# Ordering a four-layer decoder trunk on a different build-time simulation: one block around the whole trace

## The chip, the cores and the metric

The kernel runs on one core of one Trainium2 chip. The metric is the device time of one execution in microseconds (us). A time of a kernel is the median of several runs; beside it stands one profiled execution, whose trace gives a start, a duration and the releasing event of every instruction. The engines are named as the profile names them: PE (TensorE, matrix multiply), PEld (its weight load), DVE (VectorE), ACT (ScalarE), POOL (GpSimd) and SP (SyncE, which here only issues transfers). Each engine works through its own list of instructions strictly in the order of the list. Engines wait for one another by semaphores.

## The reference

A causal trunk of four layers over x of 1024 positions by 1024 channels, f32. Every layer computes `x + gate * mixer(rmsnorm(x) * (1 + scale) + shift)`, where shift, scale and gate come from `c @ ada_w[i] + ada_b[i]`. The mixers:

- layers 0 and 3: HGRN2, a gated linear recurrence with 8 heads of 128 channels. One input projection (1024 to 4096: q, f, i, z), the recurrence in chunks, an RMS norm per head, a SiLU gate, one output projection;
- layer 1: sliding-window attention (window 128), 16 query heads and 4 key heads of 64 channels, rotary embedding, QK norm, a learned sink per head, SiLU gate, output projection;
- layer 2: gated DeltaNet (GDN), 16 value heads and 8 query/key heads of 128 channels, a causal convolution of 4 taps on q, k and v, a triangular solve per chunk, norm, SiLU gate, output projection.

```
h = rmsnorm(x, norm_g[i]) * (1.0 + scale) + shift
y = (hgrn2_mixer, swa_mixer, gdn_mixer)[i % 3](h, ...)
x = x + gate * y
```

## The kernel before

**Tiling.** Everything lies channels-first: a tile has 128 channels on the partitions and 512 positions (a "half", `hf`) along the row. Each f32 operand of a big product is split in a high and a low part of a rounded type (`hi`, `lo`), and `mm3` (L215 to L220) makes one product of three matmuls: hi by hi (L218), lo by hi (L219) and hi by lo (L220). `load_w` (L176) brings a piece of a weight matrix: a transfer that SP issues into `w_raw` (L187, 3 buffers), a cast on ACT to `w_hi` (L189 or L192, 4 buffers), a subtraction on DVE to `w_lo` (L190 or L193, 4 buffers). A block of 128 output columns (`proj_fm`, tile `proj_ps`) takes two such pieces and eight products in each half. The output projections are `out_mm` (tile `outp_ps`, operands loaded by `out_load`: L1306 and L1310 issue transfers on POOL, L1314 casts `o_hi` on ACT, L1315 makes `o_lo` on DVE) and `rest` (tile `out_ps`, residual add at L572).

**Stages and loops.** A start stage (constants, x, modulation of layer 0), and then per layer the mixer over its heads or units and the output projection. HGRN2 goes over 8 heads (`mix` at L1101 has the short matmuls `lev_ps`, `o_ps`, `s_ps`), the attention over 4 groups, GDN over 8 units of two value heads. A GDN unit has an `inverse` (L787): chunk products `kk_ps` and `qk_ps`, a forward substitution of 31 steps on DVE (L837, L838), and four groups of small matmuls in `z_ps` (L866, L874 to L876, L883, L891) between which POOL copies 32-partition blocks (L860, L861, L870, L886); a `scan` over eight chunks (`ks_ps`, `w_ps`, `S_ps`), and `finish`. Beside these run the input projections of later heads or units, and a stream `side` with the modulation (`ada`) of the next layers.

**What sets the order.** `weave` (L66) draws instructions from two to four streams in shares of hand-given costs, so a program order arises. With it each instruction gets a priority number, its place in the program; `high_priority(offset=...)` moves what it encloses that many places ahead (150 for HGRN2's mix, 200 for the attention's, 150 for GDN's scan and inverse, 4000 for `burst`). `tied` (L148) and `issue_after` fix that certain instructions follow others on their engine.

This is not yet the order of the chip. When the kernel function has ended, Tile (the layer that places tiles, chooses the order and writes the semaphores) plays the whole trace once on a timing simulation. Whenever an engine of that simulation can take an instruction, Tile gives it the one with the best priority among those whose inputs and whose tile buffer are there at that simulated moment, also when a better one will be ready a little later. What each engine was given, in that sequence, is its list on the chip, and the chip doesn't deviate from it. Tile has two such simulations: CoreSim, the default, and TimelineSim, which its text calls the more detailed one, with the remark that CoreSim leaves out the fixed cost of GpSimd's elementwise instructions. Before the change every list was made on CoreSim.

Also decided by this play is which buffer of a tile's ring an allocation gets and, with that, which release a transfer waits for.

Of the kernel before, what the change touches and what calls it, by code (L numbers as in the profile page):

```python
# [10 lines left out]
F32 = mybir.dt.float32  # L11
# [9 lines left out]
P = 128  # L21
T = 1024
D = 1024
KT = D // P
HT = 512
NC = HT // P
# [21 lines left out]
def drain(g):  # L48
    for _ in g:
        pass  # L50


def chain(*gs):
    for g in gs:
        yield from g


def take(g, n):
    for _ in range(n):
        c = next(g, None)  # L60
        if c is None:
            return
        yield c
# [1481 lines left out]
@with_exitstack  # L1545
def trunk(ctx: ExitStack, tc: tile.TileContext, x, c, positions, hgrn_lb, ada_w, ada_b, norm_g,
          hg_in_w, hg_out_w, hg_onorm, sw_in_w, sw_out_w, sw_qnorm, sw_knorm, sw_sinks,
          gd_in_w, gd_out_w, gd_conv_w, gd_a_log, gd_dt_bias, gd_onorm, out, layers=(0, 1, 2, 3)):
    ins = dict(x=x, c=c, positions=positions, hgrn_lb=hgrn_lb, ada_w=ada_w, ada_b=ada_b, norm_g=norm_g,
               hg_in_w=hg_in_w, hg_out_w=hg_out_w, hg_onorm=hg_onorm, sw_in_w=sw_in_w, sw_out_w=sw_out_w,  # L1550
               sw_qnorm=sw_qnorm, sw_knorm=sw_knorm, sw_sinks=sw_sinks, gd_in_w=gd_in_w, gd_out_w=gd_out_w,
               gd_conv_w=gd_conv_w, gd_a_log=gd_a_log, gd_dt_bias=gd_dt_bias, gd_onorm=gd_onorm)
    k = Trunk(ctx, tc, ins)
    k.open_norm()
    with tc.tile_pool(name="start", bufs=1, reuse_waits="tile") as sp:
        k.setup(sp)

        x1 = [sp.tile([P, D], F32, name="x_in", tag="x_in1", bufs=NC) for _ in range(NC)]
        sq = sp.tile([P, D], F32, name="x_sq")
        x0 = [sp.tile([P, D], F32, name="x_in", tag="x_in0", bufs=NC) for _ in range(NC)]  # L1560
        k.fetch_x(0, x0)
        ada = []
        for part, bank, col in ((2, ("lev", "ada_row", 2), 0), (0, None, D), (3, ("s", "ada_row", 1), None), (1, None, None)):
            acc = sp.tile([P, HT], F32, name="ada_acc", tag="acc", bufs=3)
            ada.append((layers[0], part, acc, k.ada_load(layers[0], part), bank))
            if layers[0] == 0 and col is not None:
                k.preload(hg_in_w[0], (col,))
        rb = k.norm_stats(0, k.load_x(sp, 0, x0, sq))
        a = k.norm_apply(layers[0], 0, rb)
        for n in range(2):  # L1570
            gs = [k.ada_first(*x) for x in ada[2 * n:2 * n + 2]]
            for g in gs:
                next(g)
            k.step = k.step if n else None
            for g in gs:
                drain(g)
            drain(take(a, KT // 2))
        drain(a)
        k.start = [tc.cur_priority]
        k.fetch_x(1, x1)  # L1580
        ssq = k.load_x(sp, 1, x1, sq)
        k.spill_x(0)
        rb = k.norm_stats(1, ssq)
        k.start.append(tc.cur_priority)
        drain(k.norm_apply(layers[0], 1, rb))
        k.conv_taps(sp)
    k.level_masks()
    k.nst.close()
    for n, i in enumerate(layers):
        nxt = layers[n + 1] if n + 1 < len(layers) else None  # L1590
        k.more = nxt is not None
        side = iter(())
        if n == 0:
            side = k.ada(i, (4, 5))
        if nxt is not None:
            side = chain(side, k.ada(nxt, (0, 1, 2)), k.ada(nxt, (3, 4, 5)))
        body = (k.hgrn2, k.swa, k.gdn)[i % 3](i, side)
        for hf, t in enumerate(body):
            drain(t)
            if nxt is None:  # L1600
                k.store_x(out, hf)
            else:
                if hf == 0:
                    k.open_norm()
                a = k.norm_apply(nxt, hf, k.norm_stats(hf))
                if hf == 0:
                    drain(a)
                else:
                    k.last = a
                    k.nst.close()  # L1610


# [27 lines left out]
```

## Time and profile before

| | |
|---|---|
| median of 3 runs | 2654.2 us (2652.76 to 2654.95) |
| profiled execution, whole | 2652.67 us |
| its span, first to last instruction | 2650.9 us |
| instructions | 50785 |
| busy: PE / PEld | 2563.2 us (97%) / 2045.3 us (77%) |
| busy: DVE / ACT / POOL | 2021.3 (76%) / 1325.2 (50%) / 162.3 us (6%) |
| mean clock granted to TensorE | 0.991 |
| moved by transfers | 309.96 MB, mean 117 GB/s |

The stages in the span, read from the lines that are at work: start 0 to 72 us, HGRN2 of layer 0 to about 520, attention to about 1030, GDN from about 1100 to 2110 with its eight units until about 1910, HGRN2 of layer 3 to the end.

In a row of groups stand line, engine, operation, output<-inputs, count, then busy time and the mean of one in ns, then the idle time just before these instructions and what ended it. In a row of waits stand the waiting engine and line, what it waited for, and total, number and longest in us. In a row of windows stand the stretch, its length, and per engine busy us (number of instructions), then the granted clock, the share of the transfer engines and GB/s. Matmuls are pipelined: one counts as busy until its modelled end, while the next has long started.

### The profile page before, as it was taken

How to read it: one execution, taken by the hardware profiler on the slowest of the kernel's cores; microseconds unless marked ns; L12 is line 12 of the kernel's file. 1: busy time of each engine (PE TensorE's matmuls, PEld its weight loads, DVE VectorE, ACT ScalarE, POOL GpSimd, SP SyncE). 2: the span in 40 equal slices, each digit the busy share in tenths (PEclk: the TensorE clock that was granted, in tenths of full speed). 3: DMA queues.
4: the chain of work that ended last, by engine and by line, in shares of the span. 5: the costliest groups of instructions: out<-in, count | busy, mean ns of one | idle time of the engine just before them, and what ended most of it. 6: DMA issues, size and time to landing. Idle time of an engine off the chain costs nothing.

```text
span 2650.9 us, 50785 instructions
## 1 busy us (share of the span) xinstructions
PE 2563.2 (97%) x18271; PEld 2045.3 (77%) x18271; DVE 2021.3 (76%) x5655; ACT 1325.2 (50%) x3467; POOL 162.3 (6%) x382
## 2 busy tenths in 40 slices
PE   7999999999999999999999999999999999999998
PEld 4777777778888867777777787778788877787777
DVE  5585789777687878868899999988776837368675
ACT  4443444443464655545666666666544434245452
POOL 0001000011000000101001101110221000000010
PEclk8999999999999999999999999999999999999999
DMA  7333343544233252434343444334585312122343
GB/s 263 96 114 92 112 143 118 163 137 138 65 103 104 70 165 90 131 110 117 97 116 90 119 116 120 81 96 104 175 248 173 115 49 80 41 81 66 122 140 116
DMA packets 388369, 309.96 MB, mean 117 GB/s; under 512 B 74851, under 2 KB 314902, under 8 KB 388118
## 3 DMA queue, kind: packets, MB, share of 16 engines
q1 hardware_dynamic: 375574, 265.82, 33.9%
q0 software_dynamic: 12544, 40.90, 4.8%
q8 instruction: 144, 2.36, 0.4%
q14 instruction: 107, 0.88, 0.1%
HBM read 245.75 MB, written 60.88 MB: 116 GB/s over the span
## 4 chain that ended last, share of the span: by engine, by line
PE 73%; DVE 13%; DMA 5%; ACT 4%; issue 3%; SPq 1%; POOL 0%; DVEq 0%; ACTq 0%; POOLq 0%
PE proj_ps L220 10%; PE proj_ps L218 10%; PE proj_ps L219 10%; PE outp_ps L219 5%; PE outp_ps L218 5%; PE outp_ps L220 5%; PE projw_ps L219 2%; PE projw_ps L218 2%; PE projw_ps L220 2%; DVE gd_tb L690 1%; DVE w_lo L190 1%; PE projt_ps L219 1%; PE projt_ps L220 1%; PE projt_ps L218 1%; PE w_ps L945 1%
## 5 line engine op out<-in xcount | busy, mean ns | idle before, releaser
L218 PE MATMUL proj_ps<-hhi,w_hi 128*128 128x512 f32 x1664 | 675.2, 406 | 3.6 <-ACT gd_tb L688 3.3
L219 PE MATMUL proj_ps<-hlo,w_hi 128*128 128x512 f32 x1664 | 671.3, 403 | 0.0
L220 PE MATMUL proj_ps<-hhi,w_lo 128*128 128x512 f32 x1664 | 670.7, 403 | 0.0
L218 PEld LDWEIGHTS proj_ps<-hhi,w_hi 128*128 128x128 f32 x1664 | 314.3, 189 | 64.2 <-ACT gd_tb L688 5.9
L220 PEld LDWEIGHTS proj_ps<-hhi,w_lo 128*128 128x128 f32 x1664 | 314.0, 189 | 57.9 <-issue 0.4
L219 PEld LDWEIGHTS proj_ps<-hlo,w_hi 128*128 128x128 f32 x1664 | 314.4, 189 | 54.9 <-issue 0.9
L189 ACT CAST w_hi<-w_raw 128x512 fp32r<-128x512 f32 x352 | 214.2, 613 | 265.2 <-PE proj_ps L219 155.2
L190 DVE TENSOR_TENSOR w_lo<-w_raw,w_hi 128x512 fp32r<-128x512 f32 x352 | 236.3, 676 | 139.7 <-ACT w_hi L189 136.4
L218 PE MATMUL outp_ps<-o_hi,w_hi 128*128 128x512 f32 x576 | 229.8, 401 | 8.4 <-ACT o_hi L1314 7.1
L219 PE MATMUL outp_ps<-o_lo,w_hi 128*128 128x512 f32 x576 | 229.7, 399 | 1.5 <-DVE o_lo L1315 1.4
L220 PE MATMUL outp_ps<-o_hi,w_lo 128*128 128x512 f32 x576 | 228.4, 398 | 2.6 <-DVE w_lo L190 2.5
L192 ACT ACTIVATE w_hi<-w_raw,par 128x512 fp32r<-128x512 f32 (+1 forms) x136 | 94.9, 698 | 131.4 <-PE outp_ps L219 92.8
L690 DVE SCALAR_TENSOR_TENSOR gd_tb<-gd_xs,taps,gd_tb 128x512 f32<-128x512 f32 x192 | 145.6, 758 | 16.6 <-ACT gd_tb L688 12.4
L218 PEld LDWEIGHTS outp_ps<-o_hi,w_hi 128*128 128x128 f32 x576 | 109.5, 190 | 31.9 <-ACT o_hi L1314 8.7
L444 DVE SCALAR_TENSOR_TENSOR ada_acc<-ada_w,par,ada_acc 128x512 f32<-128x512 f32 x154 | 114.9, 746 | 20.6 <-DMA ada_w<-in_ada_w_dram 19.5
L193 DVE SCALAR_TENSOR_TENSOR w_lo<-w_raw,par,w_hi 128x512 fp32r<-128x512 f32 (+1 forms) x136 | 96.7, 715 | 43.3 <-ACT w_hi L192 40.1
L220 PEld LDWEIGHTS outp_ps<-o_hi,w_lo 128*128 128x128 f32 x576 | 109.6, 190 | 25.7 <-DVE w_lo L190 3.1
L219 PEld LDWEIGHTS outp_ps<-o_lo,w_hi 128*128 128x128 f32 x576 | 109.7, 190 | 25.2 <-DVE o_lo L1315 3.4
L1306 POOL DMA_DIRECT2D o_in<-od x72 | 38.8, 539 | 1216.7 <-DVE hg_F L1177 428.3
L219 PE MATMUL projt_ps<-w_lo,hhi 128*128 128x256 f32 x384 | 110.8, 290 | 2.1 <-DVE w_lo L190 2.1
L218 PE MATMUL projt_ps<-w_hi,hhi 128*128 128x256 f32 x384 | 110.5, 290 | 2.0 <-ACT w_hi L189 2.0
L220 PE MATMUL projt_ps<-w_hi,hlo 128*128 128x256 f32 x384 | 110.7, 290 | 0.0
(411 smaller groups left out, 5336.4 us busy)
## 6 DMA issues: line engine op xcount, KB each, us to landing
ada_w<-in_ada_w_dram SPq DMA_DIRECT2D x160, 256.0 KB, 2.8
w_raw<-in_hg_in_w_dram SPq DMA_DIRECT2D x136, 256.0 KB, 2.8
w_raw<-in_gd_in_w_dram SPq DMA_DIRECT2D x128, 256.0 KB, 2.9
o_in<-od POOLq DMA_DIRECT2D x72, 256.0 KB, 3.5
x<-xd SPq DMA_DIRECT2D x64, 256.0 KB, 4.5
w_raw<-in_gd_out_w_dram SPq DMA_DIRECT2D x64, 256.0 KB, 3.2
xd<-x POOLq DMA_DIRECT2D x48, 256.0 KB, 2.7
w_raw<-in_sw_in_w_dram SPq DMA_DIRECT2D x48, 256.0 KB, 3.0
```

The lines of the kernel that those rows point to most:

```text
L189: nc.scalar.copy(hi, raw)
L190: nc.vector.tensor_tensor(lo, raw, hi.bitcast(F32), ALU.subtract)
L192: nc.scalar.activation(hi, raw, AF.Copy, scale=scale)
L193: nc.vector.scalar_tensor_tensor(lo, raw, scale, hi.bitcast(F32), ALU.mult, ALU.subtract)
L218: mm(out, a[0], b[0], start=start, stop=False)
L219: mm(out, a[0], b[1], start=False, stop=False)
L220: mm(out, a[1], b[0], start=False, stop=stop)
L444: self.step = self.nc.vector.scalar_tensor_tensor(acc, w, c, acc, ALU.mult, ALU.add)
L690: last = nc.vector.scalar_tensor_tensor(y, xs[:, j:j + HT], w(j), y, ALU.mult, ALU.add)
L945: nc.tensor.matmul(po[:, hd[a]], dd["u"][a, hf][:, cs], rhs, start=True, stop=True)
L1306: nc.gpsimd.dma_start(t, od[(k0 + k) * P:(k0 + k + 1) * P, sl])
```

## The change

The body of `trunk` from the creation of the `Trunk` object to the last store is put inside `with tc.block(schedule_with_timeline_sim=True):`. A Tile block is traced into a basic block of its own that is entered unconditionally and ordered as a unit; with this argument Tile plays that block on TimelineSim instead of CoreSim. No instruction of the program's own is added, removed or altered, no priority, offset, share, buffer count or tie is altered, and nothing is left outside the block but the constants that are set before `trunk` is called.

```diff
-    k = Trunk(ctx, tc, ins)
-    k.open_norm()
-    with tc.tile_pool(name="start", bufs=1, reuse_waits="tile") as sp:
-        k.setup(sp)
...
+    with tc.block(schedule_with_timeline_sim=True):
+        k = Trunk(ctx, tc, ins)
+        k.open_norm()
+        with tc.tile_pool(name="start", bufs=1, reuse_waits="tile") as sp:
+            k.setup(sp)
...
+            body = (k.hgrn2, k.swa, k.gdn)[i % 3](i, side)
+            for hf, t in enumerate(body):
+                drain(t)
+                if nxt is None:
+                    k.store_x(out, hf)
                 else:
-                    k.last = a
-                    k.nst.close()
+                    if hf == 0:
+                        k.open_norm()
+                    a = k.norm_apply(nxt, hf, k.norm_stats(hf))
+                    if hf == 0:
+                        drain(a)
+                    else:
+                        k.last = a
+                        k.nst.close()
```

All other lines of the diff are the same lines, indented by four more columns.

More of the change, by code (lines that the diff above doesn't have):

```diff
@@ L1552, in trunk @@
                gd_conv_w=gd_conv_w, gd_a_log=gd_a_log, gd_dt_bias=gd_dt_bias, gd_onorm=gd_onorm)
-    k = Trunk(ctx, tc, ins)
-    k.open_norm()
-    with tc.tile_pool(name="start", bufs=1, reuse_waits="tile") as sp:
-        k.setup(sp)
[L1558 to L1586, printed above, removed]
@@ L1587, in trunk @@
-    k.level_masks()
-    k.nst.close()
[L1589 to L1607, printed above, removed]
-                else:
-                    k.last = a
-                    k.nst.close()
+    with tc.block(schedule_with_timeline_sim=True):
[3 more added lines that the diff above has]
+            k.setup(sp)
+            x1 = [sp.tile([P, D], F32, name="x_in", tag="x_in1", bufs=NC) for _ in range(NC)]
+            sq = sp.tile([P, D], F32, name="x_sq")
+            x0 = [sp.tile([P, D], F32, name="x_in", tag="x_in0", bufs=NC) for _ in range(NC)]
+            k.fetch_x(0, x0)
+            ada = []
+            for part, bank, col in ((2, ("lev", "ada_row", 2), 0), (0, None, D), (3, ("s", "ada_row", 1), None), (1, None, None)):
+                acc = sp.tile([P, HT], F32, name="ada_acc", tag="acc", bufs=3)
+                ada.append((layers[0], part, acc, k.ada_load(layers[0], part), bank))
+                if layers[0] == 0 and col is not None:
+                    k.preload(hg_in_w[0], (col,))
+            rb = k.norm_stats(0, k.load_x(sp, 0, x0, sq))
+            a = k.norm_apply(layers[0], 0, rb)
+            for n in range(2):
+                gs = [k.ada_first(*x) for x in ada[2 * n:2 * n + 2]]
+                for g in gs:
+                    next(g)
+                k.step = k.step if n else None
+                for g in gs:
+                    drain(g)
+                drain(take(a, KT // 2))
+            drain(a)
+            k.start = [tc.cur_priority]
+            k.fetch_x(1, x1)
+            ssq = k.load_x(sp, 1, x1, sq)
+            k.spill_x(0)
+            rb = k.norm_stats(1, ssq)
+            k.start.append(tc.cur_priority)
+            drain(k.norm_apply(layers[0], 1, rb))
+            k.conv_taps(sp)
+        k.level_masks()
+        k.nst.close()
+        for n, i in enumerate(layers):
+            nxt = layers[n + 1] if n + 1 < len(layers) else None
+            k.more = nxt is not None
+            side = iter(())
+            if n == 0:
+                side = k.ada(i, (4, 5))
+            if nxt is not None:
+                side = chain(side, k.ada(nxt, (0, 1, 2)), k.ada(nxt, (3, 4, 5)))
+            body = (k.hgrn2, k.swa, k.gdn)[i % 3](i, side)
[3 more added lines that the diff above has]
+                    k.store_x(out, hf)
+                else:
+                    if hf == 0:
+                        k.open_norm()
+                    a = k.norm_apply(nxt, hf, k.norm_stats(hf))
+                    if hf == 0:
+                        drain(a)
+                    else:
+                        k.last = a
+                        k.nst.close()
```

## The prediction

> **What bounds the kernel now.** I read the page first: busy times and the chain that ended last.
>
> ```profile
> span 2650.9 us, 50785 instructions
> PE 2563.2 (97%) x18271; PEld 2045.3 (77%) x18271; DVE 2021.3 (76%) x5655; ACT 1325.2 (50%) x3467; POOL 162.3 (6%) x382
> PE   7999999999999999999999999999999999999998
> DVE  5585789777687878868899999988776837368675
> PE 73%; DVE 13%; DMA 5%; ACT 4%; issue 3%; SPq 1%; POOL 0%; DVEq 0%; ACTq 0%; POOLq 0%
> ```
>
> PE is busy in nine tenths or more of 38 of 40 slices, and 73% of the chain that ended last are its matmuls. So the time is PE's work, plus the places where the next matmul in PE's list was not ready. What a new order can change are those places. The view by stretches says where they are (length, then PE, PEld, DVE, ACT, POOL):
>
> ```profile
> 0.00:72.00 72.00, 52.46 (x192) 30.89 (x193) 43.57 (x128) 33.06 (x57) 3.22 (x42) 0.87 0.74 267
> 72.00:480.00 408.00, 402.02 (x3550) 318.67 (x3549) 301.24 (x955) 167.91 (x437) 7.25 (x8) 1.00 0.38 115
> 480.00:520.00 40.00, 33.96 (x381) 25.19 (x380) 29.00 (x105) 19.25 (x46) 3.81 (x7) 0.96 0.42 136
> ...
> 570.00:660.00 90.00, 84.54 (x526) 73.75 (x525) 72.11 (x148) 38.72 (x69) 6.74 (x13) 1.00 0.38 117
> ...
> 1030.00:1120.00 90.00, 87.04 (x429) 67.65 (x428) 75.89 (x166) 53.97 (x124) 7.79 (x22) 0.98 0.33 98
> ...
> 1360.00:1850.00 490.00, 479.96 (x3405) 384.52 (x3404) 449.78 (x1325) 318.52 (x1018) 41.14 (x106) 1.00 0.40 105
> 1850.00:1910.00 60.00, 55.46 (x445) 42.56 (x444) 40.80 (x81) 33.90 (x88) 14.66 (x29) 0.94 0.53 158
> ...
> 2110.00:2500.00 390.00, 386.45 (x3479) 306.69 (x3478) 244.22 (x860) 156.41 (x418) 0.00 (x0) 1.00 0.22 68
> 2500.00:2590.00 90.00, 86.55 (x637) 68.26 (x635) 65.13 (x179) 42.00 (x96) 7.53 (x14) 0.98 0.41 134
> 2590.00:2651.00 61.00, 53.93 (x263) 43.93 (x262) 31.34 (x47) 15.24 (x24) 0.00 (x0) 0.99 0.37 123
> sum 2651.00, PE 2563.17 PEld 2045.28 DVE 2021.25 ACT 1325.20 POOL 162.29; mean PE 170.88 PEld 136.35 DVE 134.75 ACT 88.35 POOL 10.82
> ```
>
> PE's idle time is 2651.0 - 2563.2 = 87.8 us. Of it 19.5 lie in the start, where the transfer engines are 74% busy and the data sets the pace. The steady stages have little: 6.0 in layer 0's heads, 10.0 in GDN's units, 3.6 in layer 3's heads. The handovers between mixer and output projection have much for their length: 6.0 in 480 to 520, 5.5 in 570 to 660, 3.0 in 1030 to 1120, 4.5 in 1850 to 1910, 3.5 in 2500 to 2590; then 7.1 at the end.
>
> Two things follow. What an order can win is bounded by 87.8 - 19.5 = 68.3 us of visible idle, in pieces; what it can lose has no such bound, since an instruction placed too early holds all of its list. And the trace holds natural repeats: layers 0 and 3 run the same lines, and so do GDN's units, each ordered anew in the same play. Their differences price what another order of the same work is worth. For six units, cut at the last `z_ps` group of each:
>
> ```profile
> 1351.40:1436.60 85.20, 82.19 (x614) 65.87 (x612) 79.45 (x233) 55.47 (x179) 7.19 (x21) 1.00 0.40 106
> ...
> 1615.00:1701.30 86.30, 85.06 (x626) 67.65 (x625) 79.15 (x226) 54.34 (x177) 8.35 (x21) 1.00 0.39 104
> ...
> sum 534.80, PE 522.29 PEld 419.20 DVE 490.27 ACT 344.55 POOL 48.39; mean PE 87.05 PEld 69.87 DVE 81.71 ACT 57.42 POOL 8.06
> ```
>
> PE idles 3.0 us in the worst unit and 1.2 in the best; the mean is (534.8 - 522.3) / 6 = 2.1.
>
> **The change part by part.** The sum is made against the profiled execution: 2652.67 us, which is its span of 2650.9 and 1.8 around it. It stands 1.5 under the median of the runs, 2654.2, well inside their spread.
>
> Durations: the 50785 instructions stay, with their shapes and engines. Their busy times count 0.
>
> The block's edges: no instruction of the program lies outside, so nothing is kept from overlapping. Entering and leaving may cost a branch per engine, which the trace of before doesn't have. Its nearest row is the longest time for which an engine waited for issue alone at the start:
>
> ```profile
> PEld par_ps L241 <- issue: 3.7, 1, 3.7
> ```
>
> So 0 to 3.7 us; there is no gain in it, since nothing is taken away. I take 0, because the load of the start's tables and of x, 19.5 us of PE idle, covers an entry, and the end has one branch. The Trainium skill (Advanced Engine Details and Errata, Control Flow Timing) gives about 51 ns for an unconditional branch; two of them would make an estimated 0.1 us. No run here shows it.
>
> GpSimd's copies: this is the one cost that the change's own description says the present simulation leaves out. POOL's copies stand in GDN's `inverse`, before the group of small matmuls at L883. The next group, L891, has the same size and the same tie but waits for no copy:
>
> ```profile
> L883 PE MATMUL z_ps<-gd_Z,gd_uq 64*64 64x64 f32 x256 | 9.2, 220 | 7.0 <-DVE gd_uq L878 6.9
> L891 PE MATMUL z_ps<-gd_uq,gd_Z 64*64 64x64 f32 x256 | 9.2, 221 | 0.6 <-DVE gd_Z L888 0.5
> ...
> L886 POOL COPY gd_uq<-gd_Uc x16: 603/951/1142, 1247.3 to 1861.8; 32x512 f32<-32x512 f32 x16
> ...
>   PEld z_ps L883: 5.1, 3
> ```
>
> Eight groups at L883 lose 7.0 us, eight at L891 0.6. The weight load before L883 waited three times for the copy itself, 5.1 us. If the play knows that a copy lasts 0.6 to 1.1 us, it fills that time with projections and puts L883 behind them: -6.4 us. Bounds: 0 if the wait is DVE's (L878, which the profile names), -7.0 if all goes. I take -6.4.
>
> The handovers: here an operand goes `od` in HBM, POOL's transfer `o_in`, ACT's `o_hi`, DVE's `o_lo`, PE.
>
> ```profile
> POOL o_in L1306 <- DVE hg_F L1172: 12.0, 1, 12.0
> POOL o_in L1306 <- DVE hg_zs L1059: 6.9, 1, 6.9
> ...
> PE outp_ps L218 <- ACT o_hi L1314: 7.1, 3, 2.8
> ```
>
> POOL issues `o_in` in list order and waits for a free `tmp` buffer that the head's mix also takes from; in 480 to 520 it sat 12.0 and 6.9 us on that, and behind it stand the further loads. Layer 3 does the same in 2500 to 2590 with 3.5 us of idle PE instead of 6.0. So one placement of the same handover against another is worth 6.0 - 3.5 = 2.5 us (2.6 before rounding). Four handovers besides that bad one (570, 1030, 1850, 2500) can be redealt: all four as bad as layer 0's costs 4 x 2.6 = +10.4, all five at the better ratio of 3.45 to 6.04 saves 43% of (6.0 + 5.5 + 3.0 + 4.5) = 19.0, that is -8.2. I take +10.4, the end of the loss: in these short stretches PE's supply passes four engines in line, little other work is left to fill a hole, and each of the offsets that start them early counts places in an order that is no longer the same.
>
> GDN's units: DVE is busy 449.8 of 490 us (92%) and PE 480.0 (98%); two nearly full lists tied to each other leave little to absorb a changed order. All eight units as bad as the worst is (3.0 - 2.1) x 8 = +7.4 (unrounded), as good as the best (1.2 - 2.1) x 8 = -6.7. I take +7.4: with both lists this full, a wait that a new order adds lands on PE. The term holds other waits than L883's.
>
> The heads of HGRN2 and the attention: layer 0's idle share is 6.0 / 408 = 1.5%, layer 3's 0.9%. Swapped, it is worth 2.3 us either way. I take 0.
>
> Sum: 0 + 0 - 6.4 + 10.4 + 7.4 = +11.4. Forecast: 2652.67 + 11.4 = 2664 us, and 1.5 more by the median of runs: **2665 us**, 0.4% slower. Its own ends: 0 - 7.0 - 8.2 - 6.7 - 2.3 = -24 (2628 by the profiled execution) and 3.7 + 0 + 10.4 + 7.4 + 2.3 = +24 (2676), which are 2630 and 2678 by the median of runs.
>
> **The rivals.**
>
> The waits on POOL go, faster. If TimelineSim times POOL's copies and issued transfers as the chip does, the holes at L883 and at the handovers are filled:
>
> ```profile
> PE outp_ps L219 <- DVE o_lo L1315: 1.4, 3, 0.9
> ```
>
> It wins 6.4 at L883 and 7.1 + 1.4 = 8.5 at the output projection's first matmuls: -14.9, 2639 us by the median of runs. For it: just these waits are among PE's longest. Against it: the places sum to 15 us, and every other list is redealt too. It decides if GDN's units keep their mean of 2.1 us.
>
> Nothing that can be told: the gains and losses above cancel. For it: the units differ by 1.8 us at most, and redealing some thirty heads and units at random averages out. Time 2654, within 5.
>
> Weights come late, much slower. SP's list holds the weight loads among stores that wait for their producers:
>
> ```profile
> w_raw<-in_gd_in_w_dram SPq DMA_DIRECT2D x128, 256.0 KB, 2.9
> ...
> SPq L187 <- DVE w_lo L190: 560.8, 162, 36.2
> ...
> PE outp_ps L220 <- DVE w_lo L190: 2.5, 1, 2.5
> PE projt_ps L219 <- DVE w_lo L190: 2.1, 4, 1.2
> PE projt_ps L218 <- ACT w_hi L189: 2.0, 2, 1.7
> ```
>
> SP already waits long on buffer releases, and a stall of PE behind a late weight cost 0.5 us in the mean of one row (2.1 / 4) and 2.5 at the most; I price one at 1.2, the middle row's longest. If a store is dealt in front of the loads, GDN's 128 loads, 64 column blocks, can each pay 1.2 us: +77, 2731 us. It decides from the point at which a pair is issued more than one block, some 8 products in two halves, late. Against it: now these three rows, 6.6 us, are all that PE waits for weights.
>
> More room than the idle shows. Matmuls start closer than they last, so PE's busy row hides gaps:
>
> ```profile
> 1800.51 0.40 PE L218 MATMUL proj_ps<-hhi,w_hi 128*128 128x512 f32 x1
> 1800.74 0.39 PE L219 MATMUL proj_ps<-hlo,w_hi 128*128 128x512 f32 x1
> ...
> L218 PEld LDWEIGHTS proj_ps<-hhi,w_hi 128*128 128x128 f32 x1664 | 314.3, 189 | 64.2 <-ACT gd_tb L688 5.9
> ```
>
> The start interval is 0.23 us under a busy time of 0.40; gaps up to 0.17 don't show. The weight loads of this one line have 64.2 us of idle before them where its matmuls have 3.6. An order that closed two thirds of it would bring -43, 2611 us. Against it: these are gaps of tenths that come with each change from one kind of matmul to another, which no order spares. The Trainium skill (Perfetto Trace Analysis, Identifying the Most-Contended Engine) says the same of the busy row, and to judge headroom by the weight loads' busy share; by that 77%, not 97%, PE would be far from full. The trace agrees on the overlap.
>
> **How the numbers follow.** Forecast (2665) 0.42, the POOL rival (2639) 0.28, nothing 0.17, late weights (2731) 0.09, hidden room (2611) 0.04. A run of this kernel can't tell less than 0.2%, 5 us, from no change. Faster: 0.28 + 0.04, less 0.02 where the gain stays under 5 us, plus 0.02 from the forecast's lower end: 0.32. Slower: 0.42 + 0.09, less 0.02 and 0.01 at the forecast's lower end: 0.48. The rest, 0.20, is the same. The range reaches below the forecast's lower end, 2630, to 2620, half the way to the last rival, and upward from its +24 to 2720, most of the way to the late weights; what it leaves out is the rest of these two. The likeliest case alone has 2630 to 2678.
>
> **What would show it.** The stretches again: PE's idle of 19.5 in the start should stay; the five handovers should have about 33 us in all where they now have 22.5; GDN's units more than 2.1 each; L883's idle about 1. Wrong if PE's idle falls under 80 us; if `w_hi` or `w_lo` top PE's waits, the weights came late; if start, busy times or granted clock (0.87 there) change, durations were not constant.

## The result and the profile after

The changed kernel takes 3046.0 us (median of 4 runs, 3044.8 to 3047.3), the kernel before 2654.6 beside it. The ratio is **1.147, 95% interval 1.145 to 1.149**: 391 us slower, outside the range by far. The page of the changed kernel, its span, busy times, PE's busy tenths and granted clock, and the engines' shares of the chain that ended last:

```profile
span 3045.6 us, 50837 instructions
PE 2735.9 (90%) x18271; PEld 2206.7 (72%) x18271; DVE 2057.7 (68%) x5655; ACT 1323.3 (43%) x3467; POOL 158.4 (5%) x382
PE   8999899899999997888888888888977999998999
PEclk9999999899899999998889788898977999999989
PE 59%; DVE 13%; DMA 12%; issue 8%; ACT 5%; SPq 2%; POOL 1%; DVEq 0%; POOLq 0%; ACTq 0%
```

The same 18271 matmuls are there. PE's idle time is 3045.6 - 2735.9 = 309.7 us where it was 87.7, and its busy time has grown by 2735.9 - 2563.2 = 172.7 us. Together that is the whole difference of the spans, 394.7. The mean granted clock fell from 0.991 to 0.922, and the tenths show both in the same place, PE's busy share in slices 16 to 31 and the clock in 19 to 31. That is GDN. The view by stretches (start, layers 0 to 3), cut where the norm of the layer's first half starts, for layer 0 where that of its second half does, before:

```profile
0.00:64.40 64.40, 48.16 (x180) 28.16 (x181) 38.50 (x115) 26.42 (x45) 3.22 (x42) 0.87 0.74 268
64.40:576.90 512.50, 497.19 (x4207) 393.07 (x4205) 379.26 (x1158) 220.43 (x542) 19.15 (x30) 0.99 0.41 125
576.90:1034.50 457.60, 444.19 (x2861) 368.60 (x2861) 356.66 (x958) 233.18 (x561) 17.54 (x33) 0.99 0.34 107
1034.50:2050.40 1015.90, 987.27 (x6394) 788.60 (x6392) 858.53 (x2262) 599.84 (x1734) 110.53 (x255) 0.99 0.45 124
2050.40:2650.90 600.50, 586.36 (x4635) 466.86 (x4635) 388.31 (x1164) 245.33 (x588) 11.85 (x22) 1.00 0.29 91
```

and after:

```profile
0.00:57.00 57.00, 43.05 (x184) 24.91 (x185) 39.68 (x114) 26.93 (x47) 3.19 (x42) 0.94 0.82 297
57.00:628.50 571.50, 522.79 (x4235) 418.68 (x4234) 391.59 (x1164) 218.09 (x544) 19.15 (x30) 0.95 0.38 113
628.50:1126.20 497.70, 456.72 (x2855) 382.47 (x2854) 354.26 (x954) 232.31 (x559) 16.95 (x33) 0.95 0.32 99
1126.20:2435.90 1309.70, 1132.81 (x6411) 909.36 (x6410) 880.33 (x2266) 604.40 (x1736) 108.38 (x257) 0.87 0.35 96
2435.90:3045.60 609.70, 580.49 (x4594) 471.26 (x4592) 391.89 (x1158) 241.54 (x583) 10.77 (x20) 0.98 0.28 87
```

The GDN stretch is 1309.7 - 1015.9 = 293.8 us longer, three quarters of the loss: PE's busy time there grew by 145.5 us at a clock of 0.87 instead of 0.99, its idle time by 148.3. The stretch of layer 0 loses 59.0 (the start before it gains 7.4), layer 1's 40.1, layer 3's 9.2. What PE waits for (line, releaser, total us, times, longest):

```profile
PE w_ps L945 <- DVE gd_y L940: 25.8, 32, 2.5
PE S_ps L950 <- ACT gd_ws L946: 24.8, 37, 2.4
...
PE w_ps L961 <- ACT gd_wg L960: 16.2, 29, 1.3
...
PE ks_ps L934 <- DVE gd_S L956: 12.8, 18, 3.3
```

Before, the first two of these rows were

```profile
PE w_ps L945 <- DVE gd_y L940: 1.4, 1, 1.4
...
PE S_ps L950 <- ACT gd_ws L946: 1.3, 3, 0.6
```

These are the steps of GDN's `scan`: for each chunk PE makes `ks_ps`, DVE `gd_y`, PE `w_ps`, ACT `gd_ws`, PE `S_ps`, DVE `gd_S`, and only then the next chunk's `ks_ps` can start. How the list serves this chain is seen in the timeline of PE (start, us, instruction). Before, in a unit's scan:

```profile
1447.01 0.60 PE L934 MATMUL ks_ps<-gd_S,gd_k 128*128 128x256 f32 x2
1447.45 0.59 PE L935 MATMUL ks_ps<-gd_S,gd_q 128*128 128x256 f32 x2
1447.69 0.58 PE L218 MATMUL proj_ps<-hhi,w_hi 128*128 128x512 f32 x1
1448.11 0.39 PE L219 MATMUL proj_ps<-hlo,w_hi 128*128 128x512 f32 x1
1448.34 0.40 PE L220 MATMUL proj_ps<-hhi,w_lo 128*128 128x512 f32 x1
1448.57 0.40 PE L218 MATMUL proj_ps<-hhi,w_hi 128*128 128x512 f32 x1
1448.81 0.38 PE L945 MATMUL w_ps<-gd_y,gd_uq 128*128 128x128 f32 x2
...
1453.20 0.60 PE L934 MATMUL ks_ps<-gd_S,gd_k 128*128 128x256 f32 x2
```

After, where 24 projections back to back, from 1558.62 on, have just ended:

```profile
1564.41 0.39 PE L220 MATMUL proj_ps<-hhi,w_lo 128*128 128x512 f32 x1
1564.63 0.38 PE L945 MATMUL w_ps<-gd_y,gd_uq 128*128 128x128 f32 x2
...
1569.11 0.59 PE L935 MATMUL ks_ps<-gd_S,gd_q 128*128 128x256 f32 x2
1571.47 0.49 PE L945 MATMUL w_ps<-gd_y,gd_uq 128*128 128x128 f32 x2 [1.76 <-DVE gd_y L940]
1572.67 0.46 PE L945 MATMUL w_ps<-gd_y,gd_uq 128*128 128x128 f32 x2 [0.71 <-DVE gd_y L940]
1573.59 1.22 PE L950 MATMUL S_ps<-gd_ws,gd_kt 128*128 128x256 f32 x2 [0.46 <-ACT gd_ws L946]
1574.60 0.64 PE L961 MATMUL w_ps<-gd_wg,gd_uq 128*128 128x128 f32 x2
1575.60 1.19 PE L934 MATMUL ks_ps<-gd_S,gd_k 128*128 128x256 f32 x2 [0.36 <-DVE gd_S L956]
```

Before, each wait of the chain is covered by a few projections, here four in the 1.36 us from the start of the second `ks_ps` to that of `w_ps`. After, a step finds either a long run of projections ahead of it (here 24, which take 6.0 us) or none at all, and then PE stands idle between the steps, and the step's own matmuls slow down from 0.6 to 1.2 us with the clock. The order of PE's matmuls says the same for the whole of GDN: projections (input and output) that stand between two steps of one unit's chain, mean (median), 56 of each kind, and the length of a run of projections in each layer:

```
                     ks to w     w to S      S to ks    mean run of projections, layers 0 to 3
before               7.5 (5)      2.9 (3)    4.6 (4)    11.2   7.7   8.6  12.2
changed kernel       9.5 (0)      2.8 (0)    5.2 (0)    19.2  15.9  19.9  19.7
```

The amount per step is a sixth larger, 17.5 on the mean after 15.0. What changed more is how it is dealt out: the median of 5, 3 and 4 became 0, 0 and 0, a feast and a famine. Another thing moved with it: the inverse's 1792 `z_ps` matmuls, of which before none lies within a scan, lie within one in 1536 cases. Cut at the first `S_ps` and the last `gd_y` of each unit's scan, four fifths of the layer's 293.8 us are inside the scans:

```
us, worked out from the traces      before   after   difference
layer 2 until its first scan         224.6   266.6      42.0
scans of units 0 to 6                354.0   587.1     233.1
between these scans                  271.8   274.0       2.2
from the start of the last scan      165.5   182.0      16.5
```

### The profile page after: what moved, and what is told of

Its sections match the earlier page's. It is cut to its first block, busy times and chain, and to the rows that moved or that the text cites. A ratio compares the mean times of both kernels' runs of the same rounds, so it can differ in the third digit from the quotient of the medians.

```text
span 3045.6 us, 50837 instructions
## 1 busy us (share of the span) xinstructions
PE 2735.9 (90%) x18271; PEld 2206.7 (72%) x18271; DVE 2057.7 (68%) x5655; ACT 1323.3 (43%) x3467; POOL 158.4 (5%) x382
## 4 chain that ended last, share of the span: by engine, by line
PE 59%; DVE 13%; DMA 12%; issue 8%; ACT 5%; SPq 2%; POOL 1%; DVEq 0%; POOLq 0%; ACTq 0%
PE proj_ps L218 9%; PE proj_ps L219 9%; PE proj_ps L220 8%; DMA ada_w<-in_ada_w_dram 7%; PE outp_ps L218 3%; PE outp_ps L219 3%; PE outp_ps L220 3%; PE projw_ps L219 2%; PE projw_ps L220 2%; PE projw_ps L218 2%; DVE ada_acc L444 2%; DVE w_lo L190 2%; PE projt_ps L218 1%; PE projt_ps L220 1%; PE projt_ps L219 1%
## 5 line engine op out<-in xcount | busy, mean ns | idle before, releaser
L218 PE MATMUL proj_ps<-hhi,w_hi 128*128 128x512 f32 x1664 | 682.9, 411 | 34.7 <-ACT gd_tb L688 20.9
L218 PEld LDWEIGHTS proj_ps<-hhi,w_hi 128*128 128x128 f32 x1664 | 324.9, 195 | 109.3 <-ACT gd_tb L688 25.1
L220 PEld LDWEIGHTS proj_ps<-hhi,w_lo 128*128 128x128 f32 x1664 | 323.3, 194 | 66.7
L219 PEld LDWEIGHTS proj_ps<-hlo,w_hi 128*128 128x128 f32 x1664 | 324.3, 195 | 63.7 <-DVE hlo L535 0.6
L218 PE MATMUL outp_ps<-o_hi,w_hi 128*128 128x512 f32 x576 | 230.2, 407 | 19.5 <-ACT o_hi L1314 10.5
L444 DVE SCALAR_TENSOR_TENSOR ada_acc<-ada_w,par,ada_acc 128x512 f32<-128x512 f32 x154 | 115.5, 750 | 91.7 <-DMA ada_w<-in_ada_w_dram 90.6
L218 PEld LDWEIGHTS outp_ps<-o_hi,w_hi 128*128 128x128 f32 x576 | 110.7, 194 | 45.6 <-ACT o_hi L1314 14.2
L1137 ACT COPY hg_X<-hg_qf 128x384 f32<-128x384 f32 x96 | 49.7, 517 | 151.3 <-PE lev_ps L1116 80.5
L218 PE MATMUL projt_ps<-w_hi,hhi 128*128 128x256 f32 x384 | 110.5, 292 | 4.0 <-ACT hhi L534 1.8
```

Source lines behind the costliest of these rows:

```text
L218: mm(out, a[0], b[0], start=start, stop=False)
L219: mm(out, a[0], b[1], start=False, stop=False)
L220: mm(out, a[1], b[0], start=False, stop=stop)
L444: self.step = self.nc.vector.scalar_tensor_tensor(acc, w, c, acc, ALU.mult, ALU.add)
L1137: nc.scalar.copy(xv[:, :, 0:3, :], qv[:, :, 1:4, :])
```

## The experiments

Three theories were on the table. **A**: the other simulation puts long runs of ready projections in front of the chain's next step. **B**: the modulation stream (`ada`) is put in the wrong place, either its transfers (B1) or its steps on DVE (B2). **C**: that simulation has wrong durations, and the order suffers in many places at once. A' is A widened from PE's list to those of DVE and ACT, A'' narrows it to what passes GDN's scan. "Usual" and "other" below mean CoreSim and TimelineSim. All ratios are to the kernel before, with their 95% intervals; stages are cut as above, but layer 0's starts at its first norm, some 16 us into the span, so that it holds part of the start (560.5 before, 611.8 after).

**The block alone.** 

```diff
-    with tc.block(schedule_with_timeline_sim=True):
+    with tc.block():
```

> The same block around the whole trace, but ordered on the default simulation; PE's list stands in the same order as before. Theory A (the lists that the other simulation makes are the loss, because PE is handed long runs of projections ahead of the mixers' short steps): nothing is lost by the block, 2654 us within 0.2%. Rival (the block itself costs: its entry, its end, or buffers that come free only at its end): some of the 391 us is here, over 2670 us.

Measured: 2653.8 us, ratio 0.9992 (0.9982 to 1.0001), with the lists of the kernel before. The block costs nothing; what is left is the order.

**Without the modulation stream**, on both simulations. Left out is the computation of the modulation of layers 1 to 3 and of the gate of layer 0; constants stand in its place.

```diff
+        nc.vector.memset(self.mod[:, 1:, :], 0.1)
+        nc.vector.memset(self.mod[:, 0, 16:24], 0.1)
...
-            if n == 0:
-                side = k.ada(i, (4, 5))
-            if nxt is not None:
-                side = chain(side, k.ada(nxt, (0, 1, 2)), k.ada(nxt, (3, 4, 5)))
```

> Before, without the side stream: the modulation of layers 1 to 3 and the gate of layer 0 are constants instead of being computed from c and ada_w, so 144 ada_w loads and their steps on DVE are left out. It is the partner of noside_tl. DVE has some 108 us less to do (144 steps of 0.75 us), PE hardly anything less; both theories: 2600 to 2654 us.

> After, without the side stream (the same parts left out as in noside_core). Theory A (runs of projections): they are as long without the stream, 18.9 on average in GDN, so most of the loss stays: 280 us or more over noside_core. Theory B (DVE's list holds ada steps whose transfers are still under way, 105 us of such waits after against 20 before, and PE starves behind DVE): without them the loss falls under 150 us over noside_core.

Measured: 2650.2 (ratio 0.9973, 0.9963 to 0.9983) on the usual simulation, 2944.8 (1.1085, 1.1062 to 1.1107) on the other. Between the two the layers differ by +9, +7, +264 and +11 us, where the full kernels differ by +51, +40, +294 and +9. So without this stream the loss of layers 0 and 1 all but goes, and that of GDN stays: its rows, usual and then other,

```profile
1036.30:2047.60 1011.30, 985.85 (x6390) 786.41 (x6389) 829.55 (x2193) 597.83 (x1734) 106.22 (x255) 0.99 0.41 112
```

```profile
1052.90:2328.50 1275.60, 1111.01 (x6406) 889.99 (x6405) 844.55 (x2197) 605.11 (x1736) 107.27 (x257) 0.89 0.33 89
```

B holds for layers 0 and 1, not for GDN.

**Transfers or steps?** The same stream on the other simulation, but its steps read a tile that is already there; 144 weight transfers and thus the true modulation are left out.

```diff
-                wt = self.wp.tile([P, HT], F32, name="ada_w", tag="raw", bufs=RAW)
-                nc.sync.dma_start(wt, w[:, k, part * HT:(part + 1) * HT])
-                self.ada_step(acc, wt, k)
+                wt = self.adab[:, None, :64].to_broadcast([P, 8, 64])
+                self.ada_step(acc.rearrange("p (a b) -> p a b", a=8), wt, k)
```

> After, with the side stream's steps on DVE kept, but each reads a resident tile instead of a loaded piece of ada_w: 144 transfers are left out, and the modulation of layers 1 to 3 and the gate of layer 0 are of other values. Without the whole stream layers 0 and 1 lost 9 and 7 us to the other simulation, with it 51 and 40. Theory B1 (DVE's list holds steps whose transfer is still under way): without transfers the loss of layers 0 and 1 falls to under 15 us each, as without the stream; the whole is 2950 us or so. Theory B2 (the steps themselves stand in front of the mixers' work on DVE, whatever they read): it stays over 30 us each, 3000 us or more.

Measured: 3018.4, ratio 1.1353 (1.1317 to 1.1388). In the changed kernel DVE waited 90.6 us in 84 pieces for these transfers,

```profile
DVE ada_acc L444 <- DMA ada_w<-in_ada_w_dram: 90.6, 84, 3.4
```

before 19.5 in 22. With the wait gone, layer 0 gets 611.8 - 592.4 = 19 us back and layer 1 11.5. The other 32 and 29 us over the kernel before stay. As they go when the whole stream goes, they belong to what is left of it. Most of that is its 144 steps on DVE, 0.75 us each, in front of which or behind which the mixer's own work then stands (B2); its transposes, sums and short matmuls are in it too, and which of these do it was not isolated. The chain that ended last in the changed kernel has 7% of the span in these transfers; without them only 3046.0 - 3018.4 = 27.6 us came back, 0.9%, so its share is no measure of what they cost.

**Long runs of projections on the usual simulation.** The 24 matmuls of each projection bank are tied behind the bank's first and raised in priority, so that they are issued in one go.

```diff
+                if k == 0:
+                    lead = self.nc.tensor.matmul(ps, a[0], b[0], start=True, stop=False)
+                with self.burst(), self.tc.issue_after(lead.ins):
...
```

> Before, on the default simulation, with the 24 matmuls of a projection's bank made to follow its first one without a gap where their weights are there. That imitates one property of the other simulation's PE list alone: in GDN the runs of projections between other work grow from 8.6 to 21.3 on average (after: 19.9), in layer 0 from 11.2 to 15.6, in layer 3 from 12.2 to 16.2. Theory A: GDN, 1016 us from layer 2's first norm to layer 3's, grows by 150 to 300 us, the whole to 2810 to 2990 us. Theory B, and theory C (the long runs are a by-product, the loss comes from wrong durations in that simulation): under 2715 us.

Measured: 2882.0, ratio 1.0848 (1.0824 to 1.0872). GDN takes 1206.8, that is +190.9, at a granted clock of 0.91, and PE's waits are those of the changed kernel, at shifted lines:

```profile
1071.00:2277.80 1206.80, 1095.84 (x6394) 872.56 (x6393) 880.86 (x2262) 604.02 (x1734) 105.46 (x255) 0.91 0.37 104
```

```profile
PE S_ps L957 <- ACT gd_ws L953: 14.6, 32, 0.5
PE w_ps L952 <- DVE gd_y L947: 12.5, 21, 2.1
```

Long runs, with what they bring along, are **sufficient** for such a loss: nothing of the other simulation is in this kernel, and GDN loses two thirds as much. The time from `gd_y`'s end to its `w_ps`, worked out over both heads of the 56 steps, is 0.44 us before, 2.30 here, 2.32 in the changed kernel. But it is not the same loss throughout. Of the 190.9 us 137.5 lie inside the scans of units 0 to 6, where the changed kernel lost 233.1, and 49.9 between them, where that lost 2.2; and 1312 of the `z_ps` matmuls came to lie within a scan here too.

**Ties on PE.** In GDN no projection may be issued ahead of the scan's last traced matmul, on both simulations.

```diff
-                self.mm3(ps, a, (self.hhi[hf][:, k, :], self.hlo[hf][:, k, :]), k == 0, k == KT - 1)
+                with self.tc.issue_after(self.step_mm.ins) if self.step_mm else nullcontext():
+                    self.mm3(ps, a, (self.hhi[hf][:, k, :], self.hlo[hf][:, k, :]), k == 0, k == KT - 1)
...
-                    nc.tensor.matmul(po[:, hd[a]], dd["u"][a, hf][:, cs], rhs, start=True, stop=True)
+                    self.step_mm = nc.tensor.matmul(po[:, hd[a]], dd["u"][a, hf][:, cs], rhs, start=True, stop=True)
...
```

> Before, on the default simulation, with one more tie in GDN: a projection's matmuls may not stand on PE ahead of the last matmul of the scan that the program has before them. PE's runs of projections hardly alter (8.5 on average, 8.6 before). It is the partner of anchor_tl. Every theory: 2630 to 2700 us.

> After, with the same tie: on the other simulation too PE can't be handed projections far ahead of the scan's next step. GDN's runs fall from 19.9 to 12.3 on average (median 18 to 6), the other layers' stay. Theory A (the long runs are GDN's loss): GDN, 1310 us after and 1016 before, comes down by 130 us or more; the whole to 2920 us or less. Theory C (wrong durations in that simulation, the runs are a by-product): GDN keeps over 1250 us.

Measured: 2683.3 (1.0092, 1.0069 to 1.0116) and 3032.6 (1.1406, 1.1379 to 1.1434). On the other simulation GDN gave back only 15 us, 1294.9 against 1309.7, and C's number came. The theory in its simple form, PE's list alone, fell here. The tie did not thin out the steps: between `ks` and `w` stand 13.1 projections on the mean (median 12) where the changed kernel has 9.5 (0). Two things were seen besides. `gd_y` started 3.31 us after its first `ks_ps` product, against 1.77 in the changed kernel and 1.47 before, and DVE was busy with other work for 2.9 of these, so that stood ahead of the chain. And the inverse's `z_ps` matmuls, which before lie between two scans in every unit, lay within a scan, as in the changed kernel.

**Ties on three engines.** Wherever a weave mixes a mixer with other streams, these may not pass the mixers' last traced instruction on PE, DVE or ACT.

```diff
-            c = next(s[0], None)
+            with ExitStack() as behind:
+                for key in ("tensor", "vector", "scalar"):
+                    if key in LAST:
+                        behind.enter_context(tc.issue_after(LAST[key].ins))
+                c = next(s[0], None)
...
```

> The usual simulation orders the program, but wherever a weave mixes a mixer's steps with other streams (projections of the next columns, output projection, ada steps), an instruction of the other streams on TensorE, VectorE or ScalarE may not be issued before the mixer's instruction on that engine that was traced last ahead of it. So no engine's list can have other work handed ahead of the chain. It is the yardstick for the next run. Theory A' (the loss is work handed ahead of the chain): near the kernel before, since that order hands little ahead: 2640 to 2740. Theory C (the other simulation has wrong durations and the order suffers in many places): says the same of this kernel.

> The same ties on all three engines, in one block on the other simulation. Theory A' (work handed ahead of the chain on PE, DVE and ACT is the loss, and with PE's list alone tied it moved to DVE's list): the time comes to within 100 us of the run before it in this call, that is at most some 2830, and layer 2 to under 1150 (1309.7 in the changed kernel). Theory C (the order suffers wherever its simulation has wrong durations, whatever is tied): layer 2 stays over 1250 and the time over 2950. In between (2830 to 2950): the freedom is part of it and something else the rest.

Measured: 2867.9 (1.0793, 1.0772 to 1.0814) and 3168.8 (1.1927, 1.1909 to 1.1945). The usual order missed its window (2640 to 2740) under either theory: it loses 8% to the ties, so it lives on letting later work pass. On the other simulation A' was missed, and what C expected came. The difference between the simulations fell to nothing in layer 0 (615.3 and 616.0) but stayed 255.7 in GDN. The lists showed two holes: a projection was tied behind whichever mixer came last, so it could still pass the scan when that was the inverse, and the `z_ps` matmuls were not tied to the scan at all.

**Both holes closed.** Each stream stands behind all mixers listed before it, the inverse behind the scan too.

```diff
+            for n in range(1, s[6]):
+                for key in ("tensor", "vector", "scalar"):
+                    if (n, key) in LAST:
+                        behind.enter_context(tc.issue_after(LAST[n, key].ins))
...
-            st_ = [(scan(u, ds[u]), 18000, 0, 1, PR[0])]
+            st_ = [(scan(u, ds[u]), 18000, 0, 0.9 if u + 1 < U else 1, PR[0])]
```

> Yardstick for the next run, ordered by the usual simulation: as the run with ties on three engines, but a stream is tied behind the last instruction of every mixer listed before it in the weave. So the projections and ada steps are behind both the scan and the inverse, and the inverse of the next unit is itself behind the scan (whose weave share ends at 0.9, so that the inverse's last part, the z matmuls, is traced after the scan). Expected: 2860 to 2960 under either theory, since more ties cost the usual order something.

> The same ties in one block on the other simulation. The run with ties on three engines left two holes: a projection could still pass the scan if the inverse's instruction was the last traced, and the inverse's z matmuls, which the usual order puts between two scans, lay within the scan's last steps. Both are closed here. Theory A'' (what passes the scan is the loss): layer 2 within 60 us of the run before it in this call, so the time within some 120 us of it. Theory C (the order suffers from other placements too, whatever may pass the scan): layer 2 stays 150 us or more over that run.

Measured: 2928.5 (1.1027, 1.1009 to 1.1046) and 3203.1 (1.2053, 1.2027 to 1.2079). In both lists the `z_ps` matmuls now lie between the scans. GDN's rows, usual and then other:

```profile
1123.80:2281.00 1157.20, 1044.32 (x6426) 826.53 (x6424) 869.86 (x2272) 604.88 (x1741) 108.49 (x255) 0.94 0.39 109
```

```profile
1145.60:2532.30 1386.70, 1134.62 (x6460) 899.02 (x6459) 906.51 (x2272) 599.27 (x1743) 107.39 (x257) 0.89 0.33 92
```

The difference is still 229.5 us, so A'' as expected here was missed too, C's number came again, and the place of `z_ps` is not what makes this difference. Why the ties don't help can be read from the list: they keep back only work that was traced later than a step. What is traced between two steps may still be put there or later, and the usual order puts 7.2 projections on the mean (median 6.5) between `ks` and `w`, the other 11.9 (median 11). So the tie left most of the freedom in question, and the pair could not tell A'' from C as it was meant to.

**A smaller dose.** The same ties with the scan traced in the first 0.6 of its weave, so that fewer projections are traced between its steps.

```diff
-            st_ = [(scan(u, ds[u]), 18000, 0, 0.9 if u + 1 < U else 1, PR[0])]
+            st_ = [(scan(u, ds[u]), 18000, 0, 0.6 if u + 1 < U else 1, PR[0])]
```

> As the run of this order with all streams tied behind the scan, but the scan is traced within the first 0.6 of its weave instead of 0.9, so fewer projections are traced between two of its steps: in TensorE's list 5.7 instead of 7.2 on the mean between the ks and the w matmuls of a step, 2.4 instead of 4.1 between S and the next ks. Yardstick, ordered by the usual simulation: layer 2 between 1120 and 1200 (1157.2 there).

> The same trace in one block on the other simulation: 7.1 instead of 11.9 projections on the mean between ks and w, 4.3 instead of 6.3 between S and the next ks. Theory A'' (what stands in the list between two steps of the scan is the loss): the period of a scan's step falls by about the cover taken away, (4.8 + 2.0) x 0.23 = 1.6 us or more, from 11.8 to 10.2 or less, and the difference of layer 2 to the run before falls from 229.5 to under 150. Theory C (other placements): period within 0.8 us of 11.8 and difference still 180 or more.

Measured: 3024.8 (1.1399, 1.1367 to 1.143) and 3236.0 (1.2175, 1.2156 to 1.2193). GDN's rows, usual and then other:

```profile
1120.70:2375.60 1254.90, 1079.74 (x6425) 846.00 (x6424) 882.24 (x2272) 601.81 (x1741) 103.20 (x255) 0.90 0.36 100
```

```profile
1151.10:2571.60 1420.50, 1146.41 (x6460) 900.88 (x6459) 904.41 (x2272) 600.95 (x1743) 106.89 (x257) 0.88 0.32 90
```

The usual run missed its window (1120 to 1200): the projections that no longer fit into the scans go to the time between them, which grows from 347 to 485 us. The scan did what A'' says: a step's period fell from 11.8 to 9.4 us on the other simulation, below the 10.2 asked for, and the difference between the simulations followed:

```
us, worked out from the traces     difference in the scans    difference in layer 2
changed kernel - before                  233.1                     293.8
both holes closed                        198.5                     229.5
smaller dose                             141.5                     165.6
```

With the dose the scans' difference shrank by 57.0 and the layer's by 63.9. The layer's 165.6 lies between the two numbers that were expected (under 150, over 180). But the layer on the other simulation did not get faster: it went from 1386.7 to 1420.5. Its scans became 99.2 us shorter and the time between them 135.6 longer, from 330.1 to 465.7. The difference shrank because the usual order lost more, 97.7 against 33.8. So the length of a scan goes with the amount that stands between two steps; that the loss of the layer does is not shown by this pair. Nor does the period become equal: the usual order has 7.2 us per step with this trace, 2.2 less than the other's 9.4.

**The start alone** on the other simulation: all that is traced before the loop over the layers, with both halves of layer 0's first norm; the rest is on the usual one.

```diff
     k = Trunk(ctx, tc, ins)
-    k.open_norm()
-    with tc.tile_pool(name="start", bufs=1, reuse_waits="tile") as sp:
+    with tc.block(schedule_with_timeline_sim=True):
+        k.open_norm()
+        with tc.tile_pool(name="start", bufs=1, reuse_waits="tile") as sp:
...
```

> Before, with the block and the other simulation around the start stage alone (up to the masks); the layers are on the default simulation. After had its second norm of layer 0 at 57.0 us, before at 64.4. If the order of the start is what brings that, and layer 0 can use it, 2647 us (7 faster). If the block's end, behind which layer 0's first projections now have to stand, costs as much, 2650 to 2660 us. Slower than 2665 us if PE waits out the whole start.

Measured: 2662.4, ratio 1.002 (1.0009 to 1.0031). The norm of the second half starts at 53.3 us instead of 64.4, yet layer 0 ends at 585.9 instead of 576.9. The one stretch in which the other order is ahead, by 11.1 us here, gives nothing that lasts here: 20.1 us are lost again in the next 530. The time lies between the second and the third of the expected cases. As the layers stand behind the end of a block in this run, the loss can be that edge's as well as the order's; which was not followed up.

## Why the prediction was wrong

**The step that failed** is the term for GDN's units, +7.4 with ends of -6.7 and +7.4. It took the spread between the units of the old order as the price of a new order. All of these units had been dealt by the same simulation, by the same choice at each free moment, so they show how much that rule varies and nothing of what another rule does. Worse, the term said that full lists leave little to absorb a changed order, and then took a bound that assumed that they do absorb it. From the first unit's scan to the last one's the units measured +235.3 (233.1 in the scans, 2.2 between them), some thirty times the term, and the layer +293.8. PE's idle time per unit, which was to be over 2.1 us, is 17.6 in the mean of six units. The sentence that an order's loss has no bound, since an instruction placed too early holds all of its list, was the right one, and no term or rival was built on it: late weights was the only large loss considered, at +77.

**"Durations: 0"** was the second failed step, and was named as one that would show. Busy time went up by 172.7 us as the clock went down. A chain that has no cover makes gaps, the gaps lower the clock, and the lower clock stretches the chain's own matmuls and the projections after it. An estimate from the trace's clock record: PE was busy for 378.1 us at half clock, 38.7 before, and at half clock a projection starts every 0.427 us instead of every 0.227, so (378.1 - 38.7) x (1 - 0.227 / 0.427) = 159 of the 172.7 us are the clock.

**The heads of HGRN2 and the attention**, 0 within 2.3 us, cost +51.3 in layer 0, +40.1 in layer 1 and +9.2 in layer 3. Layers 0 and 3 run the same lines; layer 0 has the modulation stream beside it and layer 3 has none. The prediction took layers 0 and 3 as repeats of one another, and this difference between them was not in it.

**The copies of GpSimd** came out by their number. L883's idle time should fall to about 1, against L891's 0.6:

```profile
L883 PE MATMUL z_ps<-gd_Z,gd_uq 64*64 64x64 f32 x256 | 15.0, 302 | 1.0 <-issue 0.8
L891 PE MATMUL z_ps<-gd_uq,gd_Z 64*64 64x64 f32 x256 | 14.1, 291 | 0.4 <-DVE gd_Z L888 0.4
```

It fell from 7.0 to 1.0, so 6.0 of the 6.4. The reason, that the play now knows the length of a copy, is not shown: the same group keeps 5.9 us on the other simulation without the modulation stream and 6.6 with the ties on PE, and on the usual one it falls to 2.4 with the long runs and to 0.3 with both holes closed. As far as the runs show, the number was luck. The same row shows the price: the same 256 matmuls now take 302 ns instead of 220, and 5.8 us more in all.

**The block's edges**: 0 was right, by the plain block's 0.9992. **The handovers** should have had 33 us of idle PE in all; five windows of the same lengths, shifted to the same distance from the norms or the end, have 370.0 - 322.7 = 47.3 where 22.5 were. The direction was right and the loss 25 instead of 10, but what work falls into these windows has changed too. The term's sum was not made from its own rows: four handovers of 6.0, where the rows have 5.5, 3.0, 4.5 and 3.5, make +7.5 and not +10.4. **The start's** idle time stayed, 14.0 in the 57.0 us until the second norm against 16.2 in 64.4.

Of the rivals, *late weights* did not happen: PE waited 0.9 us for `w_lo` in one instance and has no row for `w_hi`, where the three rows before had 6.6 and a fourth, which the prediction left out, 0.4. *POOL's waits go* happened at its place, and the 8.5 of the handovers did not come. *Hidden room* is out, since the weight loads' busy share fell to 72% with the time up. The argument against it was misread, though: of the 64.2 us before L218's weight loads 57.4 stand between one projection and the next, 40 ns each, and only 6.8 at a change from another kind of matmul. *Nothing* fails on the ratio.

**What stays open.** That the play on the other simulation is the whole loss is shown by the plain block. The play gives the lists and deals out the buffers; that the loss comes by the lists alone was not tested apart. Long runs on PE, made on the usual simulation, are sufficient for a loss two thirds as large in GDN; that they are the only cause is not shown, because ties leave a difference of 166 to 256 us between the simulations in every form tried, and three of these four pairs came out by C's number. Work ahead of the chain on DVE is part of the rest, but in the changed kernel a small one: 1.77 against 1.47 us, an estimated 17 us over 56 steps. Why the other simulation fills in so much at once was not established, only that its lists do; whether its durations are wrong, as C has it, no run tested.

## What to carry to other kernels

A kernel whose serial chain is covered by independent work depends on that cover being dealt out a few instructions at a time; count, in the built list, the filler between two steps of the chain, and look at the median, not the mean. The spread between repeats under one ordering rule does not bound the effect of another rule. A simulation that is called more detailed can still make a far worse list, so the list itself is to be compared before its time is guessed.

## What the runs showed of the hardware

The granted clock falls without any long gap of PE. In the GDN stretch after the layer's second norm, the trace before has 59 gaps of PE, 25.6 us in all, and a clock of 1.00; after, 201 gaps with 165.8 us, of which 3 are 3.4 us or longer, and a clock of 0.87. The clock record of the traces has two levels, full and half. Before, half clock came in 11 stretches, 45.2 us in all; after, in 53 stretches, 475.7 us in all, each of 3.4 us or a multiple of it, but for the last, which the end cuts off. In the 3.4 us ahead of such a fall PE was idle for 57% at the median (34 to 100%), mostly in pieces; windows of the same length at full clock that no fall followed reached 51%. At half clock a projection starts 0.427 us after the one before instead of 0.227, and a 64 by 64 matmul takes 311 ns instead of 218, so that its mean went from 220 to 302 ns.

The Trainium skill (TensorE: Matmul & The Clock Gate, What's actually happening) gives the fall to half clock for an idle window of about 3.4 us. The trace agrees on that length, but a window need not be one gap: PE had 3 gaps of that length in the GDN stretch and the clock fell 32 times there, so the measurement decides. The same page's section "A second HAM failure mode: psum-queue depth-cycling" has PE idle briefly and often between groups of matmuls and the clock go up and down; with that the trace agrees.
